# How far the scores of an attention unit stand in front of its mix: three units in place of two, in a hybrid decoder layer

## The chip, the cores and the metric

One core of one Trainium2 chip runs the whole layer in one launch. The metric is the device time of one execution in microseconds (us). The kernel before took 1107.9, 1109.29 and 1108.44 us in three runs, a median of 1108.44.

## The reference

One decoder layer on a sequence of 1024 tokens and a width of 1024, in float32. Two groups of eight heads, 64 wide, read one normalised input through one combined projection; their outputs side by side go through `w_out`, and a squared-relu network of width 4096 follows.

```python
xn = rmsnorm(x, attn_norm_g)
proj = einsum('bsd,de->bse', xn, w_in)
qa, ka, va, qb, kb, vb, f_logit = split(proj, IN_SPLITS)
# q and k of both groups are normalised per head
out_a = swa_sinks_attention(qa, ka, va, sink_logits)   # window of 128, ALiBi, sinks, 2 key heads
log_f = log_sigmoid(f_logit + b_forget)
out_b = forgetting_attention(qb, kb, vb, log_f)        # causal softmax, + c[t] - c[s], c = cumsum(log_f)
x = x + concat([out_a, out_b]) @ w_out
hn = rmsnorm(x, mlp_norm_g)
x = x + square(relu(hn @ w_up)) @ w_down
```

## The kernel before, in words

**Number format.** Products must be nearly as exact as float32, and TensorE works on a rounded format. Nearly every operand is therefore split into a rounded part, made by ScalarE, and the rest, made by VectorE or GpSimd by subtraction, and a product is three matmuls (hi x hi, hi x lo, lo x hi), or two where one side is taken whole.

**Stages.** From 0 to about 60 us the first part of the projection is made, and the inputs are split. Then comes the attention stage, up to about 455 us, to which the change belongs. The output projection's end, the up and the down projection (by a scheme with seven products for eight blocks) follow up to 1107 us.

**The attention stage.** It has 48 units: 16 for the windowed group (two groups of four heads, eight blocks of 128 queries, `heads_a`, line 767), and then 32 for the forgetting group (`heads_b`, line 782): four pairs of heads p, and in each pair eight steps u, four for the first head and four for the second. A step is one head and one block `qp` of 256 queries, taken in the order 0, 2, 1, 3 (in the last head 1, 3, 0, 2). A block `qp` sees `qp + 1` pairs of key blocks, so the units differ in size.

A unit has two halves. Its *scores* (`scores_b`, line 638) are matmuls into one of two PSUM banks (tile `spb`), a reduction by VectorE that adds the decay and finds the row's extreme (`sb`, `nmb`, line 660), and the exponential on ScalarE (line 666); for the last pair the rows are scaled at once by the inverse sum (line 675). The result lies in buffers of probabilities, four for units with up to 512 keys (`NU`) and four for the others (`NS`), two to a unit of this group. Its *mix* (`mix_b`, line 686) turns the probabilities with TensorE transposes into one of three PSUM banks (`tpb`, line 702), empties each bank into a rounded part `pth` by ScalarE and a rest `ptl` by VectorE (lines 370 and 371), multiplies both with the values (`pvb`), adds the two halves of the result (`mtb`, line 720), and writes them to memory as mixed values (`mix_d`), or for the last pair straight into the operand of the output products. Pair p's second head gets its values by `prep_v` (line 634, cast at line 284), from two buffers in turn.

**What sets the order.** The program lists instructions; a scheduler with a clock of its own then settles each engine's order once and for all: at each moment an engine takes, of the instructions that are ready by that clock and have their buffers, the one with the best priority. The priority is the place in the list, and `tc.high_priority(offset=...)` moves an instruction forward by so many places. Scores, mixes and their preparations are listed with `HPA` (`prep`, line 736). `tc.issue_after(x)` keeps an instruction behind x on its engine.

`unit` (line 744) lists the scores of a unit, puts its mix on the list `pend`, and then `drain(DEPTH)` (line 740) lists the oldest mixes until `DEPTH` are left:

```python
def drain(n):
    while len(pend) > n:
        prep(pend.pop(0))

def unit(score, mix):
    got = prep(score)
    pend.append(lambda: mix(got))
    drain(DEPTH)
```

**Fillers.** Between units stands work without priority (`fill`, line 751): the projections of pairs 0 to 3, and from the 36th unit on the first half of the output products (`out_first`, line 859, tiles `po`); the table `PACE` says after how many units each may be listed. The output products read the split mixed values back from memory, in buffers that take the place of the projection's operands, and so can start only after the last projection.

**Splits.** `split_mix(e)` (line 568) has three steps for the mixed values of one pair of heads: the loads, and two halves, each with a multiplication by the inverse sums (`mixr`, line 590), a rounding, a subtraction, and two writes. `SPLITS` (line 51) names the (p, u) at which the loads are listed; the halves follow at the next two units. A half's multiplication is tied to `mixed[-1]`, the add of the mix listed last. The inverse sums of the pair before are made by `inverse_to` (line 549).

**The tail.** After the last unit, `DEPTH` mixes are on the list still. The products of the second half of two output tiles are listed among them by `beside` (line 893), each tied to the last score (`marks[-1]`) or to the end of the mix listed last (`ended[-1]`); `load_mix(6)` brings the last split's values.

Of the kernel before, what the change touches and what calls it, by code (L numbers as in the profile page):

```python
# [32 lines left out]
HPA = 5000  # L33
NU = 4
NS = 4
DEPTH = 2
LAST_CS = (slice(0, 256), slice(256, 512))

LAST = (6, 7, 0, 1, 2, 3, 4, 5)
# [9 lines left out]
)  # L49

SPLITS = ((0, 4), (0, 7), (1, 1), (1, 4), (1, 6), (2, 5), (3, 3))
BIG = 1e30


# [1 line left out]
def hybrid_layer(  # L56
# [511 lines left out]
    def split_mix(e):  # L568


        got = {}

        def load():
            for c in range(2):
                cs = slice(c * 512, (c + 1) * 512)
                m, q = got[c] = [
                    ap2.tile([P, 512], dt, tag=n, name=n, bufs=2)
                    for n, dt in (("mixr", F32), ("mixn", F32R))
                ]
                nc.sync.dma_start(m, mix_d[e][:, cs])  # L580
                for h in range(2):
                    nc.sync.dma_start(
                        q[rows_of[h], :].bitcast(F32), rd_d[2 * e + h, cs].partition_broadcast(HD)
                    )

        def make(c):
            m, q = got[c]
            lo = ap2.tile([P, 512], F32R, tag="mixs", name="mixs", bufs=1)
            with tc.issue_after(mixed[-1]):
                nc.vector.tensor_tensor(out=m, in0=m, in1=q.bitcast(F32), op=ALU.mult)  # L590
            split(q, lo, m, nc.scalar, nc.gpsimd)
            for part_, t in enumerate((q, lo)):
                nc.sync.dma_start(
                    mixs_d[e][part_][:, c * 512 : (c + 1) * 512], t.bitcast(F32)
                )

        return [load, lambda: make(0), lambda: make(1)]
# [32 lines left out]
    def load_c(p, h):  # L630
        cb = heads[p, "cb", h] = ap2.tile([P, S], F32, tag="bias", name=f"cb{p}{h}", bufs=2)
        nc.sync.dma_start(cb, c_d[2 * p + h].partition_broadcast(P))
# [103 lines left out]
    def prep(f, *a):  # L736
        with tc.high_priority(offset=HPA):
            return f(*a)
# [10 lines that stand above are left out]
    fillers = []  # L749

    def fill(rest=False):
        while fillers and (rest or fillers[0][0] <= len(marks)):
            fillers.pop(0)[1]()

    def ahead(p, u):
        if p > 3:
            return
        if u == 4:
            prep(prep_q, p)
        if u == 5:  # L760
            prep(prep_k, p, 0)
        if u == 6:
            prep(prep_v, p, 0)
        if u == 7:
            prep(prep_k, p, 1)
# [16 lines left out]
    def heads_b(p):  # L782
        for u in range(8):
            qp, h = (ORDER_END if p == 3 and u > 3 else ORDER_B)[u % 4], u // 4
            unit(lambda: scores_b(p, qp, h), lambda got, qp=qp, h=h: mix_b(got, p, qp, h))
            if u == 1:
                load_c(p, 1)
            if u == DEPTH:
                prep(prep_v, p, 1)
                if p:  # L790
                    prep(inverse_to, 6 + 2 * p, dn_b[(p - 1) % 2], 2)
                else:
                    prep(inverse_a)
            for step in [st.pop(0) for st in splitting if st]:
                step()
            if (p, u) in SPLITS:
                splitting.append(split_mix(SPLITS.index((p, u))))
                splitting[-1].pop(0)()
            ahead(p + 1, u)
            fill()  # L800
# [43 lines left out]
    def out_products(ps, w, es):  # L844
        wh, wl = w
        for e in es:
            j = e % 4
            for c in range(2):
                cs = slice(c * 512, (c + 1) * 512)
                mm(ps[c], wh[:, j, :], mh[e][:, cs], j == 0, False)  # L850
                mm(ps[c], wh[:, j, :], ml[e][:, cs], False, False)
            for c in range(2):
                cs = slice(c * 512, (c + 1) * 512)
                mm(ps[c], wl[:, j, :], mh[e][:, cs], False, j == 3)
# [26 lines left out]
    for p in range(4):  # L881
        heads_b(p)
# [10 lines left out]
    def beside(n, mark, *es):  # L893
        _, ps, w = ahead_of[n]
        with tc.issue_after(mark):
            out_products(ps, w, es)

    beside(0, marks[-1], 4, 5)
    beside(0, ended[-1], 6)
    beside(1, ended[-1], 4)  # L900
    drain(1)
# [421 lines left out]
```

## Time and profile before

| What | us |
|---|---|
| Runs: lowest, median, highest | 1107.9, 1108.44, 1109.29 |
| The profiled execution | 1108.97 |
| Its span, from the first to the last instruction | 1107.3 |
| TensorE busy with matmuls | 1087.1 |
| VectorE busy | 773.9 |
| ScalarE busy | 571.6 |
| GpSimd busy | 360.7 |

The profiled execution is one of its own, and 1.67 us lie around its span. PE is TensorE's matmuls and PEld its weight loads, DVE VectorE, ACT ScalarE, POOL GpSimd, SP the queue that issues most DMAs. In a row of the timeline stand the start, the duration, the engine, the line, the operation, out<-in, and in brackets the idle time before it with what ended it. In a row of the waits stand who waited, for whom, the sum in us, how often, and the longest. In a row of stretches stand the stretch, its length, and the busy time of the engines with the number of instructions, the granted clock of TensorE (1.00 all through), the share of the DMA engines and the GB/s; asked for one tile, it counts the instructions of that tile alone. L73 and L80 are lines of helpers for a matmul and a split, so the tiles tell such rows apart.

### The profile page before, as it was taken

The page shows a single profiled execution, that of the slowest core. Times are in us where ns is not written, and L with a number is a line of the kernel's source. Part 1 is how long each engine was busy: PE and PEld are TensorE (multiplying, and loading weights), DVE is VectorE, ACT ScalarE, POOL GpSimd, SP SyncE. Part 2 cuts the span into 40 slices and gives each one's busy share as a digit, 9 for nine tenths or more (in the row PEclk, how much of TensorE's full clock was granted, in tenths as well). Part 3 has the DMA queues.
Part 4 walks back from the last instruction along what each step waited for, and adds up shares of the span by engine and source line. Part 5 has one row for each costly group of instructions (what it writes and reads, how often), then busy time and mean ns, then how long its engine had stood idle before and what let it go on. Part 6 is the DMA issues. An engine that isn't in the chain of part 4 may idle for free.

```text
span 1107.3 us, 15672 instructions
## 1 busy us (share of the span) xinstructions
PE 1087.1 (98%) x5557; PEld 933.3 (84%) x5557; DVE 773.9 (70%) x1327; ACT 571.6 (52%) x1013; POOL 360.7 (33%) x338
## 2 busy tenths in 40 slices
PE   9999999999999998999999999999999999999998
PEld 8999998898997887777888888888888888888886
DVE  7387676666666577799768688756675877574395
ACT  5558587666666656464454535353543433333331
POOL 5662523336425544224222222322222222222100
PEclk9999999999999999999999999999999999999999
DMA  9401212314348456473554544344798786665523
GB/s 300 142 22 52 78 47 74 80 53 150 126 153 305 166 197 238 145 254 133 181 191 173 197 152 171 143 147 167 269 389 328 289 299 230 226 230 188 174 92 114
DMA packets 96078, 195.68 MB, mean 177 GB/s; under 512 B 7376, under 2 KB 19584, under 8 KB 96000
## 3 DMA queue, kind: packets, MB, share of 16 engines
q1 hardware_dynamic: 95856, 194.66, 50.3%
q8 instruction: 44, 0.72, 0.3%
q14 instruction: 34, 0.28, 0.1%
q10 hardware_dynamic: 144, 0.02, 0.0%
HBM read 141.61 MB, written 53.04 MB: 176 GB/s over the span
## 4 chain that ended last, share of the span: by engine, by line
PE 83%; DVE 7%; DMA 4%; issue 3%; ACT 2%; POOL 1%; SPq 0%; ACTq 0%; POOLq 0%; DVEq 0%
PE pd L73 27%; PE pu L73 26%; PE ps L73 11%; PE po L73 5%; PE pvb L73 3%; PE spb L73 3%; PE qps L73 3%; PE tpb L702 2%; PE sp L73 1%; DMA h<-part_d 1%; DMA wr<-in_w_b_dram 1%; PE pv L73 1%; DMA mixs_d<-mixn 1%; PE tpa L531 1%; DVE ptl L371 1%
## 5 line engine op out<-in xcount | busy, mean ns | idle before, releaser
L73 PE MATMUL pd<-hx,wx 128*128 128x512 f32 (+1 forms) x1350 | 304.9, 388 | 0.0
L73 PEld LDWEIGHTS pd<-hx,wx 128*128 128x128 f32 x1350 | 252.7, 188 | 52.2
L73 PE MATMUL pu<-bh,wu 128*128 128x512 f32 x896 | 276.5, 390 | 0.9 <-ACT wu L77 0.9
L73 PEld LDWEIGHTS pu<-bh,wu 128*128 128x128 f32 x896 | 168.2, 188 | 36.5 <-ACT wu L77 1.3
L73 PE MATMUL ps<-w,xh 128*128 128x384 f32 (+1 forms) x640 | 175.2, 344 | 1.4 <-DVE z L428 0.7
L73 PE MATMUL pu<-bl,wu 128*128 128x512 f32 x448 | 174.4, 390 | 0.8 <-DVE bl L80 0.8
L77 ACT CAST hx<-hr 128x1024 fp32r<-128x1024 f32 x56 | 59.0, 1054 | 176.5 <-PE pd L73 171.8
L80 POOL TENSOR_TENSOR wx<-wda,wx 128x1024 fp32r<-128x1024 f32 x24 | 63.8, 2659 | 197.1 <-ACT wx L77 169.4
L80 DVE TENSOR_TENSOR hx<-hr,hx 128x1024 fp32r<-128x1024 f32 x56 | 72.2, 1299 | 73.8 <-ACT hx L77 73.8
L73 PEld LDWEIGHTS ps<-w,xh 128*128 128x128 f32 x640 | 114.5, 189 | 3.4 <-ACT qkb L613 1.1
L73 PE MATMUL ps<-w,xl 128*128 128x384 f32 (+1 forms) x320 | 108.3, 340 | 0.0
L73 PEld LDWEIGHTS pu<-bl,wu 128*128 128x128 f32 x448 | 84.1, 188 | 18.9 <-DVE bl L80 1.4
L73 PE MATMUL po<-mix,wos 128*128 128x512 f32 x384 | 94.9, 396 | 1.0 <-ACT wos L77 0.7
L80 POOL TENSOR_TENSOR wu<-wus,wu 128x512 fp32r<-128x512 f32 x32 | 47.8, 1494 | 126.9 <-ACT wu L77 126.9
L73 PEld LDWEIGHTS po<-mix,wos 128*128 128x128 f32 x384 | 70.2, 188 | 15.9 <-ACT wos L77 1.3
L371 DVE TENSOR_TENSOR ptl<-tpb,pth 128x512 fp32r<-128x512 f32 (+1 forms) x80 | 49.6, 630 | 45.6 <-ACT pth L370 41.8
L80 POOL TENSOR_TENSOR wu<-wur,wu 128x512 fp32r<-128x512 f32 x32 | 44.0, 1376 | 87.1 <-ACT wu L77 87.1
L77 ACT CAST wu<-wus 128x512 fp32r<-128x512 f32 x64 | 38.4, 618 | 58.9 <-PE pu L73 56.1
L80 POOL TENSOR_TENSOR w<-wr,w 128x384 fp32r<-128x384 f32 (+1 forms) x47 | 50.5, 1087 | 50.3 <-ACT w L77 32.3
L997 DVE TENSOR_TENSOR ht<-hb 128x512 f32<-128x512 f32 x32 | 21.8, 722 | 63.4 <-ACT hb L1052 63.4
L77 ACT CAST wx<-wda 128x1024 fp32r<-128x1024 f32 x56 | 58.6, 1050 | 6.4 <-DMA wda<-in_w_d_dram 6.4
L370 ACT CAST pth<-tpb 128x512 fp32r<-128x512 f32 (+1 forms) x80 | 42.1, 544 | 36.2 <-PE pvb L73 29.6
(214 smaller groups left out, 1949.5 us busy)
## 6 DMA issues: line engine op xcount, KB each, us to landing
wda<-in_w_d_dram SPq DMA_DIRECT2D x34, 1024.0 KB, 9.2
hr<-hid_d SPq DMA_DIRECT2D x56, 512.0 KB, 5.7
wur<-in_w_u_dram SPq DMA_DIRECT2D x32, 512.0 KB, 4.3
hid_d<-ht SPq DMA_DIRECT2D x16, 1024.0 KB, 4.4
hid_d<-hb SPq DMA_DIRECT2D x16, 768.0 KB, 3.6
mix<-mixs_d SPq DMA_DIRECT2D x7, 1024.0 KB, 7.4
wr<-in_w_b_dram SPq DMA_DIRECT2D x32, 192.0 KB, 2.6
xr<-in_xT_dram SPq DMA_DIRECT2D x16, 256.0 KB, 4.9
```

The lines of the kernel that those rows point to most:

```text
L73: return nc.tensor.matmul(out, lhsT, rhs, start=start, stop=stop)
L77: hi_eng.copy(hi, src)
L80: lo_eng.tensor_tensor(out=lo, in0=src, in1=hi.bitcast(F32), op=ALU.subtract)
L370: nc.scalar.copy(hi[:, cols], pt[:, cols])
L371: nc.vector.tensor_tensor(out=lo[:, cols], in0=pt[:, cols], in1=hi[:, cols].bitcast(F32), op=ALU.subtract)
L531: nc.tensor.transpose(tp[:, hh * P : (hh + 1) * P], pts[hh // 2][:, hh % 2, c0 : c0 + P], ident)
L702: nc.tensor.transpose(tp[:, c0 : c0 + P], probs[qi][:, kb * P : (kb + 1) * P], ident)
L997: eng.tensor_tensor(out=out, in0=a, in1=b, op=ALU.subtract)
```

## The change

`DEPTH` becomes 3, so that three mixes wait on the list behind the scores listed last. What hung on `DEPTH` follows: `prep_v` of a pair's second head is listed at u == 3, while the inverse sums stay at u == 2. The last split is listed at (3, 4). In the tail, where three mixes are left now, `drain(2)` lists the first of them behind the products that are tied to the last score.

```diff
-DEPTH = 2
+DEPTH = 3
...
-SPLITS = ((0, 4), (0, 7), (1, 1), (1, 4), (1, 6), (2, 5), (3, 3))
+SPLITS = ((0, 4), (0, 7), (1, 1), (1, 4), (1, 6), (2, 5), (3, 4))
...
                 load_c(p, 1)
             if u == DEPTH:
                 prep(prep_v, p, 1)
+            if u == 2:
                 if p:
                     prep(inverse_to, 6 + 2 * p, dn_b[(p - 1) % 2], 2)
                 else:
                     prep(inverse_a)
...
     beside(0, marks[-1], 4, 5)
+    drain(2)
     beside(0, ended[-1], 6)
     beside(1, ended[-1], 4)
     drain(1)
```

## The prediction

> **What bounds the kernel now.** I read the page first, then the engines' busy time in stretches of 20 us, then counts of two kinds of matmul up to chosen moments, the waits, and last the timelines of the stretches in which TensorE stood still.
>
> ```profile
> span 1107.3 us, 15672 instructions
> PE 1087.1 (98%) x5557; PEld 933.3 (84%) x5557; DVE 773.9 (70%) x1327; ACT 571.6 (52%) x1013; POOL 360.7 (33%) x338
> ```
>
> TensorE (PE) is busy for 1087.1 of 1107.3 us and the change adds no matmul, so all that can be won is standstill, some 20 us in all. Where it lies is seen in the stretches:
>
> ```profile
> core 0: us, PE busy (x) PEld busy (x) DVE busy (x) ACT busy (x) POOL busy (x), PEclk, DMA share, GB/s
> 300.00:320.00 20.00, 20.00 (x139) 19.00 (x138) 13.16 (x35) 14.69 (x31) 7.98 (x13) 1.00 0.30 106
> ...
> 320.00:340.00 20.00, 17.26 (x114) 14.24 (x112) 15.80 (x39) 12.57 (x31) 6.04 (x10) 1.00 0.74 265
> ...
> 420.00:440.00 20.00, 17.11 (x114) 14.18 (x112) 14.65 (x36) 12.72 (x28) 7.76 (x13) 1.00 0.75 266
> 440.00:460.00 20.00, 18.42 (x93) 14.77 (x93) 13.76 (x22) 9.95 (x20) 4.12 (x8) 1.00 0.36 124
> ```
>
> The first row is the common state of the attention stage: projections and the first output products, the fillers, cover whatever the attention units wait for, and PE has 20.00 of 20 us. Two stretches have no such cover. From about 327 to 346 us the projections are over and the output products still wait for their operands (DMA share 0.74). From about 432 us the fillers are used up and the last mixes stand nearly alone. The three rows lose 2.74, 2.89 and 1.58 us, 7.2 together. The depth of the units can only matter in these.
>
> How far do the scores really stand in front of their mixes? Score matmuls (tile spb) and transposes of the mixes (tile tpb), counted up to two moments, spb first:
>
> ```profile
> 0.00:309.80 309.80, 30.02 (x134) 1.00 0.33 102
> ...
> 0.00:429.80 429.80, 57.26 (x256) 1.00 0.41 135
> ```
>
> ```profile
> 0.00:309.80 309.80, 18.84 (x119) 1.00 0.33 102
> ...
> 0.00:429.80 429.80, 39.78 (x256) 1.00 0.41 135
> ```
>
> A head pair has 64 score matmuls (6, 10, 6, 10 for the units 0, 2, 1, 3, twice) and 72 transposes (3, 11, 7, 15, twice). 134 is two pairs and 6 more: unit 0 of pair 2 has just been scored. 119 is pair 0 (72), the first half of pair 1 (36), unit 4 (3) and 8 of the 11 of unit 5. So units 5, 6 and 7 of pair 1 are still to be finished: three units, not the two of DEPTH. At 429.8 the last score is done (256 of 256) and the transposes have come to unit 4 of pair 3 (3 x 72 + 36 + 4 of 7): units 4, 5, 6, again three, besides the last one itself. Order is settled by the scheduler's own clock and by which buffer is free; DEPTH only places the mixes in the list that gives the priorities. The limit that holds is the probabilities' buffers, four of each kind (NU, NS), two to a unit, small and large units in turn: a score needs the buffers of the unit four before it.
>
> ```profile
> DVE sb L660 <- PE tpb L702: 9.1, 7, 2.3
> ...
> PE tpb L702 <- DVE ptl L371: 4.4, 5, 1.4
> ...
> PE spb L73 <- DVE nmb L660: 1.4, 3, 1.0
> ```
>
> The first row is that limit: the scores' reductions on VectorE (DVE) waited 9.1 us for transposes of an older unit to give up the buffer. The second is PE in the mixes: the next transposes wait until a bank is emptied, 4.4 us in five waits. The third is PE in the scores, waiting for a reduction.
>
> **The change, part by part.**
>
> *DEPTH.* The number of instructions stays. In the list, the scores of unit n now stand ahead of mix n-3, behind mix n-4; they stood ahead of mix n-2, behind mix n-3. The buffers of unit n come free with the transposes of mix n-4, so the new list asks for what the counts show already. PE work saved: none. I cost it at 0, hidden by the fillers in the common state; bounds follow in the rivals, since in the two bare stretches an order that changes by a few instructions can gain or lose.
>
> *The other splits come one mix earlier.* A split's two halves are tied to the mix that was listed last (mixed[-1]). With DEPTH 3 that is one mix older for the six splits that stay in place. One of them, split 4, has its halves here on DVE:
>
> ```profile
> 326.05 0.69 DVE L590 TENSOR_TENSOR mixr<-mixr,mixn 128x512 f32<-128x512 f32 x1
> ...
> 330.73 0.69 DVE L590 TENSOR_TENSOR mixr<-mixr,mixn 128x512 f32<-128x512 f32 x1
> 331.34 0.68 DVE L660 CUSTOM_DVE_ANT_0 sb<-spb,cb 128x512 f32<-128x512 f32 x1
> ...
> 331.95 1.27 DVE L255 TENSOR_REDUCE ss<-sq 128x8 f32<-128x512 f32 x2
> 333.14 0.61 DVE L660 CUSTOM_DVE_ANT_0 sb<-spb,cb,nmb 128x384 f32<-128x384 f32 x1
> ...
> 337.67 0.41 DVE L284 CAST vb<-qkb 128x512 fp32r<-128x512 f32 x1
> ```
>
> ```profile
> 330.70:345.70 15.00, 12.20 (x71) 8.64 (x70) 14.28 (x40) 10.17 (x25) 6.49 (x11) 1.00 1.02 403
> ```
>
> ```profile
> 333.90 0.47 PE L73 MATMUL spb<-k1b,q1b 128*128 128x512 f32 x1 [0.97 <-DVE nmb L660]
> ...
> 340.12 0.66 PE L702 MATMUL tpb<-ident,sb 128*128 128x128 f32 x4 [1.07 <-DVE ptl L371]
> ...
> 426.40 1.25 PE L702 MATMUL tpb<-ident,sb 128*128 128x128 f32 x7 [1.40 <-DVE ptl L371]
> ...
> 437.86 1.15 PE L702 MATMUL tpb<-ident,sb 128*128 128x128 f32 x6 [1.29 <-DVE ptl L371]
> ```
>
> From 330.7 to 345.7 DVE is busy for 14.28 of 15 us: here it is DVE that sets the pace. The half at 330.73 takes the place of the one at 326.05, and that one moves back to the mix before, under full cover. From 330.73 to the next start at 331.34 are 0.61 us, and the reductions behind it are the ones for which PE stands still 0.97 us. So 0.6 us goes, at the least 0 (if the stretch ends by the loads anyway) and at the most 0.6. ScalarE's rounding, GpSimd's subtraction and the two DMAs of that half move with it and are no one's wait there.
>
> *prep_v a unit later* (u == 2 to u == 3). Its cast is the row at 337.67, and it waits for the last mix of the pair before it to give up a values' buffer. It is ready no later than now, and it falls behind one score unit and one mix in the list. The mixes need it only from unit 4 on. Between 0 and 0.34 us (337.67 to the next start, 338.01) would leave the crowded stretch; since it can run only after that mix either way, I take 0. The inverse of the sums keeps its place (u == 2): 0.
>
> *The last split, (3, 3) to (3, 4).* Its halves run at units 5 and 6 in place of 4 and 5, and the mix listed last there is, with one more in hand, the same as before: that of unit 2, and of unit 3. Its loads (two of the mixed values, four of the inverses) are listed one unit later on the SP queue, where loads are issued in turn:
>
> ```profile
> 402.16 0.32 SPq L580 DMA_DIRECT2D mixr<-mix_d  x1
> ...
> 415.36 0.34 SPq L580 DMA_DIRECT2D mixr<-mix_d  x1
> ```
>
> ```profile
> 427.19 0.68 DVE L590 TENSOR_TENSOR mixr<-mixr,mixn 128x512 f32<-128x512 f32 x1
> ...
> 434.81 0.41 DVE L720 TENSOR_TENSOR mtb<-pvb,tmpb 64x256 f32<-64x256 f32 x1
> 435.14 0.67 DVE L590 TENSOR_TENSOR mixr<-mixr,mixn 128x512 f32<-128x512 f32 x1
> ...
> 438.43 0.42 DVE L720 TENSOR_TENSOR mtb<-pvb,tmpb 64x256 f32<-64x256 f32 x1
> ```
>
> ```profile
> 439.91 0.37 SPq L832 DMA_DIRECT2D mix<-mixs_d  x1
> ```
>
> ```profile
> 444.70 1.66 PE L73 MATMUL po<-mix,wos 128*128 128x512 f32 x6
> ```
>
> The two loads of mixed values went out 25 and 20 us ahead of the multiplies that use them (427.19, 435.14), which covers a unit's delay. The second multiply stands right behind the add of its mix (434.81), so the mix is what starts it; the reload goes out at 439.91, and six products on PE at 444.70 are, by their place between two units, the ones that use it or run beside it. The mix being the same, I cost the move at 0. It is a chain with little to spare, and a rival below prices it.
>
> *drain(2) in the tail.* One more mix is left after the last score, and drain(2) lists it behind the twelve products of `beside(0, marks[-1], 4, 5)` and ahead of those tied to ended[-1]. The later ties so name the same mix (unit 5) as before. Mixes have the higher priority in either place: 0.
>
> **The sum.** The profiled execution took 1108.97 us, its span 1107.3 and 1.67 around it; the median of the three runs is 0.53 lower, 1108.44. -0.6 + 0 + 0 + 0 + 0 = -0.6: 1108.4 for a profiled execution, 1107.8 against the median. About 0.2%, 2.2 us, is what a measurement of this kernel can tell from no change, so this is "the same".
>
> **Rivals.**
>
> *A: the scores' work leaves the tail (faster).* If the last unit's reductions and row scalings come earlier, the transposes no longer wait for a bank behind them: the waits of 1.40 and 1.29 us go. 0.6 + 2.7 = 3.3: 1105.1. If all five waits went, 4.4 + 0.6 = 5.0: 1103.4. For it: both waits fall where scores and evictions share DVE. Against it: the last unit's buffers come from unit 3, whose transposes are the ones waiting at 426.40, so its scores can hardly come sooner than its mixes let them.
>
> *B: scores ahead of evictions (slower).* The list now prefers the next scores to a mix that PE could finish. On DVE this looks like:
>
> ```profile
> 415.30 1.56 DVE L675 TENSOR_SCALAR sb<-sb,dnb 128x896 f32<-128x896 f32 x1
> ...
> 418.22 1.14 DVE L371 TENSOR_TENSOR ptl<-tpb,pth 128x384 fp32r<-128x384 f32 x2
> ...
> 419.46 1.79 DVE L675 TENSOR_SCALAR sb<-sb,dnb 128x1024 f32<-128x1024 f32 x1
> ...
> 432.68 0.62 DVE L675 TENSOR_SCALAR sb<-sb,dnb 128x768 f32<-128x768 f32 x1
> ```
>
> ```profile
> 416.06 0.96 ACT L370 CAST pth<-tpb 128x384 fp32r<-128x384 f32 x2
> ```
>
> ```profile
> 415.36 4.60 PE L73 MATMUL po<-mix,wos 128*128 128x512 f32 x19
> ...
> 429.68 3.01 PE L73 MATMUL po<-mix,wos 128*128 128x512 f32 x12
> ```
>
> ScalarE has both inputs of the two evictions ready at 417.0, and the evictions start at 418.22, behind a scaling of scores and what follows it. It costs nothing there, since 4.60 us of output products run on PE. Were both scalings (1.56 and 1.79, from start to next start 1.48 and 1.71) put ahead of an eviction once the products end, at 432.7, PE would stand 3.2 us longer: 1107.8 + 3.2 = 1111.0. It decides from the point where the last unit's scalings fall behind 432.7; now the last of them starts just there, at 432.68. [...]
>
> *C: the last split really is later.* If its second half were tied to the next mix, the add at 438.43 in place of 434.81, its reload would come 3.6 us later, and nothing but a few products stands between: at most 1108.44 + 3.6 = 1112.0.
>
> *D: nothing moves at all*, since the buffers decide; that differs from the forecast by the 0.6 alone and goes with it.
>
> **How the numbers follow.** The forecast with D has 0.50: 0.42 of it within 0.2%, 0.05 faster and 0.03 slower, for orders that shift by a wait or two. A has 0.29: more is to be had in the bare stretches than to lose, but the buffer speaks against it. B has 0.15, since the cover is there except at the very end. C has 0.06. So faster 0.05 + 0.29 = 0.34, same 0.42, slower 0.03 + 0.15 + 0.06 = 0.24. The range runs from A with all its waits, 1103.4, to C with none of the gain, 1112.0. The likeliest case alone has 1106.2 to 1110.6.
>
> **What would show it.** Right: the counts at the end of the last score again leave three units open; the half of split 4 stands ahead of 320 us; the waits of PE for ptl stay near 4.4 us; from 460 us on both traces run alike, shifted by under 2 us. Wrong: four units open at that moment (the depth does act); the stretch from 420 to 460 loses much less than 4.5 us (A) or much more (B); products waiting for the load of the last split (C); or a new wait where the first stage hands over to the second, where five small buffers are asked for and four exist.

## The result, and the profile after

The changed kernel takes 1109.92 us, a median of 22 runs, beside 1108.13 of 22 runs of the kernel before. The ratio is 1.0014, with a 95% interval from 1.0008 to 1.0020: about 1.6 us slower. The prediction had 1107.8, and a gain of 0.6. The profiled execution's span is 1108.0 us.

```profile
span 1108.0 us, 15674 instructions
PE 1086.6 (98%) x5557; PEld 933.6 (84%) x5557; DVE 775.6 (70%) x1327; ACT 571.4 (52%) x1013; POOL 363.0 (33%) x338
```

The page tells nothing of it; the stretches do. Busy time of the engines in stretches of 20 us, of the kernel before (rows that were not shown yet), PE first:

```profile
120.00:140.00 20.00, 20.00 (x132) 19.30 (x131) 10.43 (x37) 10.87 (x33) 10.78 (x11) 1.00 0.35 102
...
180.00:200.00 20.00, 19.23 (x122) 17.05 (x121) 13.01 (x34) 15.90 (x37) 9.81 (x9) 1.00 0.33 93
...
340.00:360.00 20.00, 19.46 (x104) 15.56 (x105) 10.95 (x27) 12.44 (x26) 12.20 (x15) 1.00 0.74 267
```

and of the changed kernel:

```profile
120.00:140.00 20.00, 19.23 (x125) 18.06 (x125) 13.42 (x45) 15.74 (x46) 10.05 (x10) 1.00 0.40 120
...
180.00:200.00 20.00, 18.41 (x105) 14.40 (x105) 15.55 (x43) 16.78 (x42) 9.80 (x9) 1.00 0.42 125
...
320.00:340.00 20.00, 19.26 (x130) 16.89 (x129) 14.51 (x37) 11.92 (x29) 5.44 (x9) 1.00 0.46 164
340.00:360.00 20.00, 18.61 (x108) 14.68 (x108) 12.69 (x32) 15.31 (x32) 10.18 (x13) 1.00 0.81 289
...
420.00:440.00 20.00, 16.97 (x113) 13.98 (x112) 13.62 (x37) 12.49 (x29) 8.81 (x13) 1.00 0.74 256
440.00:460.00 20.00, 18.14 (x95) 14.59 (x96) 12.97 (x21) 9.39 (x20) 4.12 (x8) 1.00 0.32 112
```

The bare stretch from 320 to 360 us did gain: TensorE (PE) stands still for 0.74 + 1.39 = 2.13 us where it was 2.74 + 0.54 = 3.28, and gets 238 instructions through in place of 218. What was lost was lost where the prediction saw cover, in the windowed group: 0.77 us at 120 to 140, and at 180 to 200 standstill doubles and only 105 instructions run in place of 122. Another 0.81 us is lost behind it, at 220 to 240, where the kernel before stood still for nothing. The tail is nearly as it was.

The lead of the scores is what it was. Matmuls of scores, then transposes of mixes, up to the last score:

```profile
0.00:429.90 429.90, 58.49 (x256) 1.00 0.41 135
```

```profile
0.00:429.90 429.90, 40.85 (x256) 1.00 0.41 135
```

Again all 256 scores and 256 of the 288 transposes are done. PE's waits fell a little in the mixes and rose a little in the scores:

```profile
PE tpb L702 <- DVE ptl L371: 3.4, 6, 1.3
PE spb L73 <- DVE nmb L660: 1.9, 3, 1.1
```

**A theory.** Put the two timelines of PE side by side around the forget gates, whose transpose is `ptf` and whose sum is `off`. Both take one of the three PSUM banks (tag `tr`) that the mixes turn in too. Kernel before, rows of these users alone:

```profile
107.67 0.60 PE L531 MATMUL tpa<-ident,sa 128*128 128x128 f32 x4
...
123.54 0.27 PE L457 MATMUL ptf<-ident,zt 128*64 128x128 f32 x1
...
127.57 0.27 PE L73 MATMUL off<-cum,before 64*64 64x1 f32 x2
127.77 1.09 PE L531 MATMUL tpa<-ident,sa 128*128 128x128 f32 x8
```

Changed kernel:

```profile
100.95 0.60 PE L531 MATMUL tpa<-ident,sa 128*128 128x128 f32 x4
...
120.17 0.27 PE L457 MATMUL ptf<-ident,zt 128*64 128x128 f32 x1
...
120.94 0.27 PE L73 MATMUL off<-cum,before 64*64 64x1 f32 x2 [0.33 <-DVE cum L459]
121.15 1.53 PE L531 MATMUL tpa<-ident,sa 128*128 128x128 f32 x12
```

Before, four mixes (units 0 to 3, the last at 107.67) turn ahead of the gates, and the next waits until 127.77. After, it is three, the last at 100.95, and unit 3 waits until 121.15. That is the order in which the list names them. Counted off both traces, all 551 transposes and sums in these banks follow the list, apart from 7 and 8 places where the transposes of banks that are open at once run among each other. So the three banks are given out in the order of the list, and a mix that is listed behind a preparation (the turning of queries `ptq` and keys `ptk`, the gates, the inverse sums) waits until that preparation has its bank, whatever the preparation itself waits for. The gates wait for a chain of small steps on VectorE (lines 440 to 452) that is listed without priority: in the changed kernel its input is complete at 80.1 us, but it runs from 111.5 to 118.2, and the transpose follows at 120.17. `DEPTH` sets how many mixes stand behind each of them. The same at the keys of pair 0's second head; before:

```profile
186.65 0.60 PE L531 MATMUL tpa<-ident,sa 128*128 128x128 f32 x4
...
189.07 0.60 PE L299 MATMUL ptk<-ident,qkb 128*64 128x128 f32 x4
...
195.69 0.23 PE L73 MATMUL spb<-mask_b,ident_b 128*128 128x128 bf16 x1
195.73 0.59 PE L73 MATMUL ps<-w,xh 128*128 128x384 f32 x2
```

and after:

```profile
188.17 0.60 PE L299 MATMUL ptk<-ident,qkb 128*64 128x128 f32 x4
...
190.17 0.62 PE L531 MATMUL tpa<-ident,sa 128*128 128x128 f32 x4
...
198.88 0.23 PE L73 MATMUL spb<-mask_b,ident_b 128*128 128x128 bf16 x1
198.92 0.59 PE L73 MATMUL ps<-w,xh 128*128 128x384 f32 x2
```

Mix 13 starts at 190.17 in place of 186.65, behind the keys and no longer ahead of them. The scores of the first forgetting units need the buffers of the windowed mixes, this one's among them, and the last matmul for the third of these units starts at 198.88 in place of 195.69. The projection of pair 2 (`ps`) starts right behind it: 195.73 and 198.92. The stretch without fillers, between the projections of pairs 1 and 2, grows from 5.5 us (190.2 to 195.7) to 10.6 (188.3 to 198.9). What pair 0's keys wait for here is not a projection, since that of pair 0 ended at 130.4 us in the changed kernel; in the list they stand behind mixes 11 and 12.

Two rivals. *Rival 1*: at the change from the windowed to the forgetting group, the deeper list asks for five small buffers of probabilities where four exist. *Rival 2*: any new list shuffles the whole order, and a loss or a gain falls anywhere.

### The profile page after: what moved, and what is told of

The parts are those of the page before. It is cut to its first block, busy times and chain, and to the rows that moved or that the text cites. A ratio compares the mean times of both kernels' runs of the same rounds, so it can differ in the third digit from the quotient of the medians.

```text
span 1108.0 us, 15674 instructions
## 1 busy us (share of the span) xinstructions
PE 1086.6 (98%) x5557; PEld 933.6 (84%) x5557; DVE 775.6 (70%) x1327; ACT 571.4 (52%) x1013; POOL 363.0 (33%) x338
## 4 chain that ended last, share of the span: by engine, by line
PE 81%; DVE 8%; DMA 4%; issue 3%; ACT 2%; POOL 1%; SPq 0%; DVEq 0%; ACTq 0%; POOLq 0%
PE pd L73 27%; PE pu L73 26%; PE ps L73 11%; PE po L73 5%; PE spb L73 3%; PE pvb L73 3%; PE tpb L702 2%; DMA xr<-in_xT_dram 1%; PE sp L73 1%; DMA xq<-in_x_dram 1%; PE pv L73 1%; DVE ptl L371 1%; DMA h_d<-h 1%; PE tpa L531 1%; DVE ss L255 1%
## 5 line engine op out<-in xcount | busy, mean ns | idle before, releaser
L73 PEld LDWEIGHTS ps<-w,xl 128*128 128x128 f32 x320 | 60.3, 188 | 0.5
```

Source lines behind the costliest of these rows:

```text
L73: return nc.tensor.matmul(out, lhsT, rhs, start=start, stop=stop)
```

## The experiments

Standstill is the length of a stretch less PE's busy time, in us. The last column, in us too, is the time from the start of the first score matmul (`sp`) to the end of the last (`spb`) in the profiled execution.

| Kernel | Median | Ratio to before, 95% interval | 100-140 | 180-200 | 320-360 | scores |
|---|---|---|---|---|---|---|
| before | 1108.13 | 1 | 0.00 | 0.77 | 3.28 | 370.1 |
| changed | 1109.92 | 1.0014 [1.0008, 1.0020] | 0.77 | 1.59 | 2.13 | 371.3 |
| b3_only | 1104.84 | 0.9971 [0.9963, 0.9979] | 0.00 | 0.76 | 2.15 | 366.5 |
| a3_only | 1112.20 | 1.0037 [1.0025, 1.0049] | 0.77 | 1.63 | 3.31 | 373.5 |
| k_ahead | 1106.38 | 0.9987 [0.9978, 0.9996] | 0.76 | 0.30 | 2.14 | 368.6 |
| gates6 | 1109.10 | 1.0008 [1.0000, 1.0017] | 0.00 | 1.73 | 2.25 | 371.8 |
| both | 1106.01 | 0.9983 [0.9974, 0.9992] | 0.00 | 0.20 | 2.12 | 368.6 |
| split4 | 1107.12 | 0.9996 [0.9987, 1.0005] | 0.00 | 0.56 | 2.16 | 369.6 |
| prepv | 1108.14 | 1.0001 [0.9992, 1.0010] | 0.00 | 0.92 | 3.28 | 370.4 |
| b3_preps | 1110.65 | 1.0028 [1.0017, 1.0039] | 0.00 | 0.62 | 3.01 | 372.0 |
| a1_b3 | 1104.78 | 0.9969 [0.9956, 0.9981] | 0.00 | 0.00 | 2.12 | 366.0 |
| b4 | 1107.31 | 0.9990 [0.9981, 0.9999] | 0.00 | 0.79 | 2.69 | 369.4 |
| own_bank | 1113.77 | 1.0049 [1.0037, 1.0062] | 0.00 | 0.00 | 2.34 | 366.3 |
| own_bank2 | 1103.67 | 0.9963 [0.9950, 0.9977] | 0.00 | 0.00 | 3.10 | 368.4 |

**The change cut in two.** `b3_only` has depth 2 while the windowed group is listed and 3 from the first head pair on; `a3_only` the reverse.

```diff
# b3_only, from the changed kernel
-        drain(DEPTH)
+        drain(depth[0])
...
+    depth = [2]
...
     heads_a(1)
+    depth[0] = DEPTH
# a3_only, from the kernel before
-        drain(DEPTH)
+        drain(depth[0])
...
+    depth = [3]
...
     heads_a(1)
+    depth[0] = DEPTH
+    drain(DEPTH)
```

> Depth 2 while the windowed group is listed, 3 from the first head pair on; the rest as in the changed kernel. Theory (turning banks): the three tr banks are granted in the order of the list, so a deeper list puts one more mix behind each preparation that also turns (q, k, gates); what was lost at 110 to 130 and 180 to 200 us was lost by mixes of the windowed group behind the gates and behind the keys of pair 0. It expects TensorE's standstill at 100 to 140 us back at 0 (0.8 in the changed kernel), at 180 to 200 back at 0.8 (1.6), and a time 2 to 3.5 us under the changed kernel's, 1106.5 to 1108. Rival 1 (five small buffers asked where four exist at the handover): the scores of the third forgetting unit still stand ahead of the last windowed mix in the list, so 180 to 200 stays at 1.6 and the time near 1109.5. Rival 2 (any new list shuffles the order, losses fall anywhere): no stretch returns to its old value.

> Depth 3 in the windowed group alone, 2 from the first head pair on, splits and values as before the change. Theory (turning banks): keeps the losses at 100 to 140 (0.8) and 180 to 200 (1.6), and has the stretch from 320 to 360 as before the change (3.3): 1110 to 1111.5. Rival 1: the list is back at two mixes at the handover, so 180 to 200 is at 0.8 and the time within 1 us of the kernel before. Rival 2: anything within 2 us of either.

The stretch from 180 to 200 in b3_only, then in a3_only:

```profile
180.00:200.00 20.00, 19.24 (x123) 17.22 (x122) 13.53 (x36) 15.81 (x37) 10.11 (x10) 1.00 0.34 99
```

```profile
180.00:200.00 20.00, 18.37 (x106) 14.37 (x105) 15.46 (x43) 16.76 (x42) 9.79 (x9) 1.00 0.42 125
```

Each stretch does in its half what it does in the whole. b3_only, 123 instructions, has lost nothing in the windowed group and keeps the gain at 320 to 360; a3_only, 106, has the losses and not the gain. Depth 3 is worth -0.29% in the forgetting group and +0.37% in the windowed one; together +0.08%, beside +0.14% measured. (b3_only has the splits, `prep_v` and the tail of the changed kernel too.) b3_only is under the range that I had given it, a3_only above: the effects are larger than the standstills alone. The last column has them: about 3.5 us less, and 3.5 us more, than the kernel before. Standstill misses part of it, since PE's busy time differs too, for the same 5557 matmuls: 1087.1 us before, 1084.1 in b3_only. Rival 1 falls: a3_only is back at two mixes at the handover and loses all the same. b3_only is faster than both kernels.

**The windowed group's two places.** `k_ahead` and `gates6` each move one mix ahead of one preparation in the changed kernel, `both` does both.

```diff
# k_ahead
             if g:
+                if i == 7:
+                    drain(2)
                 ahead(0, i)
# gates6
-            if (g, i) == (0, 5):
+            if (g, i) == (0, 6):
                 forget_gates()
```

> The changed kernel with one mix more listed ahead of the keys of pair 0's second head (drain(2) at the last windowed unit), so that mix 13 gets its turning bank before them. Theory: 180 to 200 returns to 0.8, the filler after it starts about 3 us earlier (195.7 in place of 198.9), 100 to 140 keeps 0.8; time 1107.5 to 1108.5. Rival 1: no return, since the buffers asked for are the same: 1109.5 to 1110. Rival 2: anything.

> The changed kernel with the forget gates listed a unit later, at unit 6, so that mix 3 is again ahead of their two turning banks. Theory: 100 to 140 returns to 0 (0.8), the stretch without fillers at 120.3 to 124.2 us goes; 180 to 200 keeps 1.6; time about 1 us under the changed kernel's, 1109. Rival 1: no change at either. Rival 2: anything.

> The changed kernel with both repairs, the gates a unit later and one more mix ahead of the keys at the end of the windowed group; depth 3 elsewhere. Theory: the two repairs add, 3.5 us (k_ahead against the changed kernel) and 0.8 (gates6): 1105.6, near b3_only's 1104.8; 100 to 140 at 0, 180 to 200 at 0.3 to 0.8, 320 to 360 at 2.1. Rival 2: does not add.

Timeline of k_ahead on PE, and the stretch from 100 to 140 in gates6:

```profile
188.41 0.60 PE L531 MATMUL tpa<-ident,sa 128*128 128x128 f32 x4
190.01 0.60 PE L299 MATMUL ptk<-ident,qkb 128*64 128x128 f32 x4
...
194.47 0.59 PE L73 MATMUL ps<-w,xh 128*128 128x384 f32 x2
```

```profile
100.00:140.00 40.00, 40.00 (x260) 38.87 (x259) 26.49 (x89) 24.98 (x76) 15.84 (x15) 1.00 0.21 67
```

In k_ahead mix 13 is ahead of the keys again (188.41, 190.01), and the filler starts at 194.47 in place of 198.92. One place in the list gives back 3.5 us, 1109.92 to 1106.38, two more than the standstill there, twice what the change had cost, and below the 1107.5 that I had expected at the least. gates6 restores its own stretch and leaves the other as it was; its median is 0.8 us lower, which the two intervals, overlapping, do not tell from nothing. With both, 1106.01 and both stretches mended; the sum of the two, 1105.6, is within the interval, but so is k_ahead alone, and in the last column the two are alike (368.6). So the keys' place costs time; what the gates' place costs, beyond the standstill, is not settled. Both together do not reach b3_only's 366.5: a part of the windowed group's loss seems to lie at places that were not looked for. Rival 2 falls for these places: three edits at chosen spots mended just those spots. What does move elsewhere is smaller: k_ahead also ended the 0.81 us that the changed kernel lost at 220 to 260.

**Where the gain comes from.** Four more kernels, on parts of the change and on b3_only.

```diff
# split4, from the kernel before
-SPLITS = ((0, 4), (0, 7), (1, 1), (1, 4), (1, 6), (2, 5), (3, 3))
+SPLITS = ((0, 4), (0, 7), (1, 1), (1, 4), (1, 5), (2, 5), (3, 3))
# prepv, from the kernel before
-            if u == DEPTH:
+            if u == 3:
                 prep(prep_v, p, 1)
+            if u == DEPTH:
# b3_preps, from b3_only
+            if u in (4, 5, 7):
+                drain(2)
             ahead(p + 1, u)
# b4, from b3_only
-DEPTH = 3
+DEPTH = 4
...
-            if u == DEPTH:
+            if u == 3:
                 prep(prep_v, p, 1)
```

> The kernel before with the fifth split listed one unit earlier, (1, 5) in place of (1, 6), and nothing else. The prediction's own step: VectorE loses one multiplication at 330.7, TensorE's standstill at 320 to 360 goes from 3.3 to 2.7, the time falls by 0.6 us to 1107.6. Theory (preparations move into the bare stretch): a split turns nothing, so 320 to 360 stays within 0.4 of 3.3 and the time within 1 us of the kernel before. Rival 2 (any new list shuffles the order): changes of 1 us and more at places that have nothing to do with the split.

> The kernel before with prep_v listed at u == 3 in place of u == 2, and nothing else: that part of the change alone. The prediction and the theory both expect nothing (0 to -0.3 us), 320 to 360 at 3.0 to 3.3, 180 to 200 at 0.8. Rival 2 expects shifts of 1 us and more somewhere, since VectorE's and ScalarE's orders change in many places.

> b3_only (depth 2 in the windowed group, 3 after), with the list drained to two mixes ahead of each preparation of the next pair's queries and keys (units 4, 5 and 7 of a pair), so that the preparations get their turning banks no earlier than in the kernel before. Theory: the gain of b3_only came from preparations that stand one mix earlier and so fall into the bare stretch at 327 to 346; here they do not, 320 to 360 goes back from 2.15 to about 3.3 with some 218 instructions of TensorE in place of 232, and the time to 1107 to 1108. Rival (the scores themselves gain by standing one unit further ahead): stays at 1104.8. Rival 2: anything.

> b3_only with depth 4 after the windowed group. Theory: the preparations of the next pair stand another mix earlier, but they need their projection, which is not sooner, while another mix waits behind them, and the buffers of four units are all asked for: 320 to 360 stays near 2.1 or falls by up to 0.5, the stretches at 230 to 300 lose 1 to 2 us more: 1104.5 to 1107. Rival (the scores' distance itself is the gain): 1102 to 1103.

prepv is worth nothing, as forecast. split4 takes 1.1 us of standstill from 320 to 360, to 2.16, where the theory had expected it to stay within 0.4 of 3.3: here the prediction's step (2.7) held, and more than held, and the theory's did not. Its time is 0.9 us lower, which its interval does not tell from nothing. Transposes of queries and keys (line 299) in the bare stretch, in the kernel before, b3_only and b3_preps:

```profile
326.00:347.00 21.00, 0.00 (x0) 1.00 0.94 356
```

```profile
326.00:347.00 21.00, 2.98 (x16) 1.00 0.92 341
```

```profile
326.00:347.00 21.00, 0.00 (x0) 1.00 0.86 321
```

In b3_only, 16 of pair 3's 24 turns, with all that hangs on them on VectorE and ScalarE, run in this window, 12 of them ahead of the first output product. Drained to two mixes ahead of each preparation, none does, and the standstill goes back to 3.01. So the order of the list puts preparations into the bare stretch, as it puts them ahead of mixes in the windowed group. That this is what makes the gain is not shown, since b3_preps undoes more than it was meant to. At the last projection product b3_only has done 155 score matmuls and 143 transposes of mixes, the kernel before and b3_preps alike 151 and 137: the units themselves stand further back again. And the second half of split 4 starts at 320.6 us in b3_only, at 327.8 in b3_preps, so that its writes fall among the loads that the output products wait for. Issues of the SP queue (`mix<-mixs_d` is one of these loads, `mixs_d<-` a write of the split), in the kernel before and in b3_only:

```profile
326.80 0.90 SPq L832 DMA_DIRECT2D mix<-mixs_d  x2
327.75 0.46 SPq L593 DMA_DIRECT2D mixs_d<-mixn  x1
...
328.94 0.42 SPq L593 DMA_DIRECT2D mixs_d<-mixs  x1
```

```profile
323.32 0.32 SPq L593 DMA_DIRECT2D mixs_d<-mixs  x1
...
327.01 1.64 SPq L834 DMA_DIRECT2D mix<-mixs_d  x3
```

In the five kernels with such writes among the loads (before, prepv, a3_only, split4, b3_preps) the first weights land 16.5 to 17.9 us after the last projection product, and the first output product starts 18.3 to 20.3 us after it. In the nine others it is 15.0 to 16.1 us, and 17.4 to 17.7 (19.2 in gates6, whose clock had fallen there, to 0.92 and 0.74 in two stretches of 5 us, see below). So there are three candidates for the gain: the preparations' place, how far the units have come at the end of the projections, and the split's writes. No run was made to separate them. The sum was not met: b3_preps is at 1110.65 where 1107 to 1108 was expected. It stands still 0.97 us at 220 to 260 and 1.90 at 260 to 300, 2.87 together, where the kernel before has 0.93. Why the half-drained list loses there was not looked into. b4 took 1107.31, a little over the 1104.5 to 1107 expected: with a list that is one unit deeper still, 2.5 us of the gain are gone. It does not speak against the second candidate, since its units had not come further: 150 score matmuls and 129 transposes were done at the last projection product. It has the first and the third, 12 turns ahead of the first output product and the split's writes ahead of the loads, and that was not enough; this points to the second without testing it by itself.

**Depth 1 in the windowed group.**

```diff
# a1_b3, from b3_only
-    depth = [2]
+    depth = [1]
```

> b3_only with depth 1 in the windowed group. Theory: the mixes of the windowed group stand one further ahead of the gates and of pair 0's preparations; 100 to 140 is at 0 already and has nothing to give, 180 to 220 may fall from 0.9 towards 0.3: 0 to 0.6 us under b3_only, 1104.2 to 1104.8. Rival (scores need their distance): the scores come too late for their mixes and the loss at 60 to 200 rises by 1 us and more.

The standstill at 180 to 220 goes from 0.92 to nothing, and the time stays (1104.84, 1104.78): 260 to 300 now stands still for 1.33 us in place of 0.51.

**A bank of its own.** If a mix waits because it shares its banks with preparations, the sharing can be ended: two banks for the mixes, one (`tq`) for everything else.

```diff
# own_bank, from the changed kernel
-        pt = pa.tile([P, 512], F32, tag="tr", name=name, bufs=3)
+        pt = pa.tile([P, 512], F32, tag="tq", name=name, bufs=1)
# the same for ptf, off and ptn; for tpa and tpb:
-            tp = pa.tile([P, 512], F32, tag="tr", name="tpb", bufs=3)
+            tp = pa.tile([P, 512], F32, tag="tr", name="tpb", bufs=2)
# own_bank2, from own_bank
+        turns.append(name)
+        own = len(turns) % 3 == 0 or len(turns) > 8
-        pt = pa.tile([P, 512], F32, tag="tq", name=name, bufs=1)
+        pt = pa.tile([P, 512], F32, tag="tq" if own else "tr", name=name, bufs=1 if own else 2)
```

> The changed kernel with the three turning banks divided: two for the mixes, one for the preparations, the gates and the inverse sums. Theory (one set of banks, granted in the order of the list, makes a mix wait behind a preparation that waits for a projection): now no mix waits for a preparation, mixes follow their scores sooner and the stretch without fillers at 188.0 to 198.6 us falls to 5 or 6 us; two banks in place of three cost in the bare stretches, where mixes go bank by bank: 320 to 360 and 420 to 460 may lose 1 to 4 us more. 1107 to 1113, its sum open; what tells is 180 to 200. Rival 2 (shuffling): 180 to 200 as before, at 1.6.

> own_bank, but the first eight turns of the windowed group's queries and keys take the three banks in turn (two of every three from the mixes' two banks), since with a bank to themselves the fillers stood still from 76.5 to 89.1 us, which cost 6.9 us more there than in the kernel before. Theory: 60 to 100 goes from 7.1 back to 0.3 to 1.5, 100 to 220 stays at 0, 320 to 360 near 2.3 and 420 to 460 near 4.9; 1113.8 less 5.6 to 6.8 is 1107.0 to 1108.2, under the changed kernel's time at the same depth of three and with one bank less for the mixes. Rival 2 (shuffling): 100 to 220 loses 1 us and more again.

own_bank at 180 to 200:

```profile
180.00:200.00 20.00, 20.00 (x129) 18.69 (x129) 14.85 (x40) 14.30 (x37) 6.45 (x8) 1.00 0.14 47
```

At depth 3, the standstill from 100 to 260 us is gone altogether, with one bank less for the mixes. Counted off PE's timeline, the windowed units' mixes now begin 9 us after their scores end, in the median of 16, where it was 27 in the changed kernel and 25 before. own_bank is at 1113.77, just over the 1107 to 1113 expected. What it loses it loses at its start, where the first queries and keys go one by one through a single bank; own_bank2 lets the first eight turns use all three. PE from 76 to 90 us, own_bank and own_bank2:

```profile
76.00:90.00 14.00, 6.90 (x32) 5.99 (x31) 9.64 (x27) 9.01 (x24) 11.50 (x13) 0.71 0.34 99
```

```profile
76.00:90.00 14.00, 13.74 (x92) 13.28 (x91) 10.26 (x42) 10.78 (x40) 9.52 (x10) 1.00 0.34 100
```

That gives 1103.67, 10 us under own_bank (5.6 to 6.8 were expected) and 0.37% under the kernel before: the lowest median of all, though its interval overlaps b3_only's. Its 320 to 360 is at 3.10, but the bare stretch itself is as in b3_only (17.6 us, 2.1 of them standstill); the other 1.0 us falls behind the first output products. Where its 4 us lie is not clear: the last column has only 1.6 of them.

## Why the prediction was wrong, point by point

- *Failed: "I cost it at 0, hidden by the fillers in the common state"*, the step on `DEPTH`. It took the buffers of probabilities for the only limit and the fillers for a cover that is always there. The turning banks are given out in the order of the list as well, and so `DEPTH` decides which mixes wait behind which preparations. And the fillers are tied to the last score: when a late mix keeps a score waiting, it keeps the cover waiting too. The runs put the step at -0.29% (with the splits in it) and +0.37%, both larger than the whole forecast. The loss is shown to come from the order of the banks, at the keys of pair 0 above all; what makes the gain stays open.
- *Failed: "The depth of the units can only matter in these"*, the two bare stretches. There is a third, between the projections of pairs 1 and 2, 5.5 us long; the row of 180 to 200 with its 0.77 us of standstill was in the view that I quoted from, and I passed it by.
- *Right: the lead of the scores.* Three units were open at the last score, before and after. That DEPTH did not move it was right; that it then moved nothing did not follow.
- *Right in place, its size not settled: the other splits, -0.6 us.* Split 4's halves are at 316.00 and 325.53 in the changed kernel, as foreseen:

```profile
316.00 0.69 DVE L590 TENSOR_TENSOR mixr<-mixr,mixn 128x512 f32<-128x512 f32 x1
...
325.53 0.69 DVE L590 TENSOR_TENSOR mixr<-mixr,mixn 128x512 f32<-128x512 f32 x1
```

  split4 alone measured -0.9 us, with an interval from -1.4 to +0.6. One part of the step is doubtful: the half's two DMAs "are no one's wait there". They are issued among the loads of the output products; in the nine kernels that have no such writes there, the first weights land 15.0 to 16.1 us after the last projection product, in place of 16.5 to 17.9 in the five that have them.
- *Right: prep_v, 0* (prepv, +0.1 us with an interval of 1 us either way).
- *Nearly right: the last split and drain(2), 0.* The tail stands still for 4.89 us in place of 4.47. In it the products do wait for the last split's load now, as rival C had it, but for 0.29 us and not 3.6:

```profile
438.83 1.14 PE L702 MATMUL tpb<-ident,sb 128*128 128x128 f32 x6 [1.31 <-DVE ptl L371]
...
445.89 1.66 PE L73 MATMUL po<-mix,wos 128*128 128x512 f32 x6 [0.29 <-DMA mix<-mixs_d]
```

- *Rivals A and B did not happen.* Of the two waits in the tail that A would have ended, one fell from 1.40 to 0.88 us and the other stayed (1.29, now 1.31). Evictions did not fall further behind scores: PE's wait for them, over the whole run, fell from 4.4 to 3.4 us. So evictions that wait behind scores were not what made the change slower.
- *The sign that I had named for being wrong*, a new wait where the groups change over, came true at that place and with another cause. The five small buffers were not it (a3_only).

## What to carry to other kernels

If buffers of one tag are given out in the order of the list, then moving one user in the list moves everyone behind it: look through all users of every tag that a step passes, and ask what each of them waits for. A cover that is tied to the covered work is not a cover for delays of that work. A depth that helps in one stage and hurts in another is two changes; cutting it in two turned 1.6 us lost into 3.3 us won, and giving the mixes banks of their own, once the first turns could use all three, won 4.

## What the runs showed of the hardware

TensorE's granted clock fell in own_bank. A transpose stood 4.75 us behind VectorE's work on the bank before it (`q1a`), and the clock behind it was 0.70, 0.50 and 0.77 in three stretches of 5 us:

```profile
81.97 1.05 PE L299 MATMUL ptq<-ident,q 128*128 128x128 f32 x4 [4.75 <-DVE q1a L292]
```

```profile
80.00:85.00 5.00, 1.48 (x6) 1.11 (x6) 3.21 (x8) 2.96 (x7) 4.13 (x4) 0.70 0.26 74
85.00:90.00 5.00, 4.20 (x19) 3.93 (x19) 3.54 (x15) 4.22 (x15) 3.55 (x4) 0.50 0.30 94
90.00:95.00 5.00, 5.00 (x29) 4.96 (x29) 2.96 (x10) 2.81 (x8) 0.00 (x0) 0.77 0.14 41
```

In the kernel before, with no wait of PE over 1.4 us in the attention stage, the rows of that stage show 1.00 all through. The wait in own_bank cost more than its length, since the work behind it was slower: a score matmul `sp<-k2z` of 128x256 took 0.41 us at 84.95, and 0.28 at 104.04, where the row of 100 to 120 us shows 1.00 again. That may be why own_bank2 won more, 10 us, than the standstill of 6.84 us that it removed from 60 to 100 us; that was not tested by itself.

In gates6 the granted clock was below 1 in the bare stretch too, with no wait as long as that:

```profile
340.00:345.00 5.00, 3.86 (x22) 2.90 (x22) 4.85 (x17) 4.21 (x9) 2.53 (x4) 0.92 1.02 410
345.00:350.00 5.00, 4.92 (x27) 3.73 (x26) 2.34 (x7) 2.80 (x8) 1.30 (x5) 0.74 1.03 400
```

PE's longest wait there was 1.10 us, at 342.99. The changed kernel has the same row, as busy and with the same wait, at full clock:

```profile
340.00:345.00 5.00, 3.86 (x25) 2.90 (x25) 4.85 (x17) 4.20 (x9) 2.52 (x4) 1.00 1.02 411
```

So with the same stillness the clock was down in one execution and not in another, and what decides it stays open. In gates6's profiled execution the bare stretch took 19.2 us in place of 17.7, about 1.5 us longer, and the whole 1110.32, above gates6's median of 1109.10. But nine of its eleven executions show a mean clock of 0.999 or 1.000, with a median of 1109.07, which speaks against the clock as the reason that gates6 gained so little. split4's profiled execution has such a place at 330 to 335 us, with 0.66.
